# RMS norm with ReLU on one core: two pairs of transfers merged, and the work of VectorE and ScalarE rearranged around them

**Chip, cores, metric.** One core of one Trainium2 chip (trn2). The metric is the device time of one execution in microseconds (us), as the median of several runs. The span in a profile, from the first to the last instruction of the core, is about 1.3 us shorter than the time of the same run (157.9 against 159.28 us). All runs quoted here were at a granted clock of 1.000.

## The reference

```python
def reference(x, gamma, eps):              # x: 16 x 1024 x 512 float32, gamma: 512, eps: 1e-5
    rms = np.sqrt(np.mean(x ** 2, axis=-1, keepdims=True) + eps)
    x_norm = x / rms * gamma
    return np.maximum(x_norm, 0).astype(np.float32)
```

16384 rows of 512 floats go in and out: 33.55 MB each way, 67.11 MB in all.

## The kernel before

Each of the 128 partitions gets 128 rows, in 8 chunks of K = 16 rows; a group is G = 8 rows. The kernel keeps six chunks in memory on the chip ("slots"); chunks 6 and 7 take the places of chunks 0 and 1 once these are stored. SyncE issues all loads (L) and stores (S) of x and the result on one queue, in the order listed. A chunk's rows lie next to each other in device memory, so a transfer of r rows per partition moves as 128 packets of r x 2 KB (the packet records of this kernel: 512 of 16 KB, 1280 of 32 KB and 256 of 64 KB for 16 transfers).

```python
    order = [(L, 0, G), (L, G, G)] + [(L, i * K, K) for i in range(1, nslots)] + [
        (S, 0, K), (S, K, K), (L, room, K), (L, room + K, K),
        (S, 2 * K, 2 * K), (S, 4 * K, 2 * K), (S, room, K),
        (S, room + K, G), (S, room + K + G, G)]
    # ... SyncE, before each transfer m of the list:
        if kind == S:
            if order[m - 1][0] == L:
                nc.sync.wait_ge(*((tick, 6) if a == 0 else (done, 10)))
            nc.sync.wait_ge(done, (a + r) // G)
        elif a >= room:
            take(nc.sync, sems[order.index((S, a - room, r))], 16)   # room is free
        transfer(m)
```

ScalarE sums the squares of each row and takes roots, one group per turn of a loop of 16 (ring indices cut):

```python
        nc.scalar.wait_ge(ready, 1)                    # a group has landed
        for j in range(G):
            a = nc.scalar.activation(out=junk[:, j, :], in_=..., func=ACTF.Square, accum_out=ss[...])
        a.then_inc(sa, 1)
        nc.scalar.wait_ge(sa, 1)
        nc.scalar.activation(out=rms[...], in_=ss[...], func=ACTF.Sqrt,
                             bias=eps_sb, scale=inv_d).then_inc(sq, 1)
        nc.scalar.sem_inc(sa, -1)
        nc.scalar.sem_inc(ready, -1)
```

VectorE treats chunks 0 to 2 in a loop by group (cut), chunks 3 to 7 in long passes, one product with the reciprocals and one with gamma that also clamps at zero:

```python
    for first, last in ((3, 3), (4, 5), (6, 7)):
        nc.vector.wait_ge(sq, per * (last + 1 - looped))
        whole(nc.vector.reciprocal, ...)               # for chunks first..last
        nc.vector.wait_ge(sv, steps)
        for i in range(first, last + 1):
            blk = here(i * K, K)
            whole(nc.vector.tensor_tensor, out=blk, in0=blk, in1=rstd[...], op=ALU.mult)
            nc.vector.wait_ge(sv, steps)
            r = G if i == nchunks - 1 else K
            for a in range(i * K, (i + 1) * K, r):
                nc.vector._custom_dve(dve_ops.TENSOR_MUL_SAT, ...).then_inc(done, r // G)
```

## Time and profile before

| | before |
|---|---|
| median time | 159.34 us (159.28 to 159.47, 3 runs) |
| span of the profiled run | 157.9 us |
| VectorE (DVE) / ScalarE (ACT) busy | 86% / 55% of the span |
| queue of x and result (q1) busy on 16 DMA engines | 99.0% of the span |
| VectorE's last work ends | 150.54 us after the start of the span |

### The profile page before, as it was taken

The page shows a single profiled execution, that of the slowest core. Times are in us where ns is not written, and L with a number is a line of the kernel's source. Part 1 is how long each engine was busy: PE and PEld are TensorE (multiplying, and loading weights), DVE is VectorE, ACT ScalarE, POOL GpSimd, SP SyncE. Part 2 cuts the span into 40 slices and gives each one's busy share as a digit, 9 for nine tenths or more (in the row PEclk, how much of TensorE's full clock was granted, in tenths as well). Part 3 has the DMA queues.
Part 4 walks back from the last instruction along what each step waited for, and adds up shares of the span by engine and source line. Part 5 has one row for each costly group of instructions (what it writes and reads, how often), then busy time and mean ns, then how long its engine had stood idle before and what let it go on. Part 6 is the DMA issues. An engine that isn't in the chain of part 4 may idle for free.

```text
span 157.9 us, 770 instructions
## 1 busy us (share of the span) xinstructions
DVE 135.2 (86%) x76; ACT 86.3 (55%) x273; POOL 0.8 (0%) x6
## 2 busy tenths in 40 slices
DVE  0015999999999999999979999999999999999910
ACT  0298739989988988988920198898600000000000
POOL 1000000000000000000000000000000000000000
DMA  7999999999999999999999999996998969999997
GB/s 257 429 494 415 398 448 473 407 398 473 456 398 398 473 456 398 398 473 456 398 398 456 465 407 398 531 531 266 531 432 365 531 299 498 398 398 415 436 411 332
DMA packets 2313, 67.12 MB, mean 425 GB/s; under 512 B 261, under 2 KB 261, under 8 KB 265
## 3 DMA queue, kind: packets, MB, share of 16 engines
q1 hardware_dynamic: 2304, 67.11, 99.0%
q10 hardware_dynamic: 8, 0.01, 0.0%
q14 instruction: 1, 0.00, 0.0%
HBM read 33.56 MB, written 33.55 MB: 425 GB/s over the span
## 4 chain that ended last, share of the span: by engine, by line
DVE 44%; ACT 27%; issue 6%; ACTq 4%; DVEq 0%; POOLq 0%
ACT junk L137 26%; DVE slots L191 22%; DVE slots L174 22%; ACTq L137 3%; ACTq L132 1%; DVE rstd L174 0%; ACT rms L142 0%; ACTq L142 0%; ACTq L145 0%; DVEq L187 0%; POOLq L124 0%
## 5 line engine op out<-in xcount | busy, mean ns | idle before, releaser
L137 ACT ACTIVATE junk<-slots 128x512 f32 x128 | 74.4, 581 | 21.5 <-POOLq L124 17.0
L191 DVE CUSTOM_DVE_ANT_1 slots<-slots,gamma_sb 128x8192 f32<-128x8192 f32 (+1 forms) x6 | 43.5, 7269 | 0.6
L174 DVE TENSOR_TENSOR slots<-slots,rstd 128x8192 f32<-128x8192 f32 x5 | 43.4, 8689 | 0.1
L160 DVE SCALAR_TENSOR_TENSOR slots<-slots,rstd,gamma_sb 128x512 f32 x48 | 32.3, 747 | 0.9 <-DVE rstd L155 0.9
L137 ACT ACTIVATION_READ_ACCUMULATOR junk<-slots x128 | 23.9, 187 | 0.0
L167 DVE TENSOR_SCALAR slots<-slots x6 | 13.8, 2294 | 0.2
L148 DVE LOAD_MASK_SELECT gamma_sb<-gseed x1 | 0.0, 14 | 8.4 <-DMA gseed<-in_gamma_dram 8.4
L142 ACT ACTIVATE rms<-ss,eps_sb x16 | 4.8, 301 | 1.8
L155 DVE RECIPROCAL rstd<-rms x6 | 1.2, 196 | 4.3 <-ACT rms L142 4.3
L130 ACT ACT_TABLE_LOAD x1 | 1.3, 1283 | 3.6 <-issue 3.6
L174 DVE RECIPROCAL rstd<-rms 128x32 f32<-128x32 f32 (+1 forms) x3 | 0.9, 314 | 0.9 <-ACT rms L142 0.9
L148 DVE STREAM_SHUFFLE gamma_sb<-gseed 128x512 f32<-128x512 f32 x1 | 0.7, 716 | 0.0
L119 POOL MEMSET gseed<- 128x512 f32 x1 | 0.5, 526 | 1.5 <-POOLq L95 1.5
L220 POOL MEMSET const-bfloat16-1.0<- 128x1 bf16 x1 | 0.1, 103 | 0.0
L220 POOL MEMSET const-uint8-127<- 128x1 uint8 x1 | 0.1, 102 | 0.0
L220 POOL MEMSET const-float32-0.0<- 128x1 f32 x1 | 0.1, 100 | 0.2 <-issue 0.2
L220 POOL MEMSET const-float32-1.0<- 128x1 f32 x1 | 0.1, 100 | 0.0
L120 POOL MEMSET eps_sb<- 128x1 f32 x1 | 0.1, 99 | 0.0
## 6 DMA issues: line engine op xcount, KB each, us to landing
slots<-in_x_dram SPq DMA_DIRECT2D x7, 4096.0 KB, 29.4
out_dram<-slots SPq DMA_DIRECT2D x3, 4096.0 KB, 15.0
slots<-in_x_dram SPq DMA_DIRECT2D x2, 2048.0 KB, 9.6
out_dram<-slots SPq DMA_DIRECT2D x2, 2048.0 KB, 7.1
out_dram<-slots SPq DMA_DIRECT2D x2, 22.2
gseed<-in_gamma_dram ACTq DMA_DIRECT2D x1, 8.0 KB
```

Source lines behind the costliest of these rows:

```text
L119: nc.gpsimd.memset(gseed, 0.0).then_inc(sem_z, 1)
L130: nc.scalar.preload_act_table(ACTF.Sqrt)
L132: with nc.scalar.Fori(0, ngroups) as gi:
L137: a = nc.scalar.activation(out=junk[:, j, :], in_=slots[:, bass.ds(base + j * d, d)], func=ACTF.Square, accum_out=ss[:, bass.ds(col + j, 1)])
L142: nc.scalar.activation(out=rms[:, bass.ds(col, G)], in_=ss[:, bass.ds(col, G)], func=ACTF.Sqrt, bias=eps_sb, scale=inv_d).then_inc(sq, 1)
L148: nc.vector.stream_shuffle(gamma_sb, gseed, [0] * 32)
L155: nc.vector.reciprocal(out=rstd[:, bass.ds(col, G)], in_=rms[:, bass.ds(col, G)]).then_inc(sv, 1)
L160: r = nc.vector.scalar_tensor_tensor(out=row, in0=row, scalar=rstd[:, bass.ds(col + j, 1)], in1=gamma_sb, op0=ALU.mult, op1=ALU.mult)
L167: nc.vector.tensor_scalar_max(out=blk, in0=blk, scalar1=0.0).then_inc(done, 1)
L174: emit(**kw).then_inc(sv, 1)
L191: nc.vector._custom_dve(dve_ops.TENSOR_MUL_SAT, out=blk, in0=blk, in1=gamma_sb[:, None, :].to_broadcast([P, r, d]), s0=float("inf"), s1=0. ...
L220: nc = _bacc.Bacc("TRN2", target_bir_lowering=False, num_devices=1)
```

## The change

Its intent is to move the same bytes in fewer, longer packets: chunks 4 and 5 are loaded by one transfer (64 KB packets instead of 32), and chunk 7 is stored by one (32 KB instead of 16). The rest: reciprocals of chunks 4 and 5 apart, ScalarE scales the last 8 rows of chunk 7 in VectorE's stead, and ScalarE's loop loses two semaphore steps. The diff, cut to its core:

```diff
-    order = [(L, 0, G), (L, G, G)] + [(L, i * K, K) for i in range(1, nslots)] + [
+    order = [(L, 0, G), (L, G, G)] + [
+        (L, K, K), (L, 2 * K, K), (L, 3 * K, K), (L, 4 * K, 2 * K),
         (S, 0, K), (S, K, K), (L, room, K), (L, room + K, K),
-        (S, 2 * K, 2 * K), (S, 4 * K, 2 * K), (S, room, K),
-        (S, room + K, G), (S, room + K + G, G)]
+        (S, 2 * K, 2 * K), (S, 4 * K, 2 * K), (S, room, K), (S, room + K, K)]
 ...  (ScalarE: table load ahead of gamma's copy, eps under its own semaphore)
-                func=ACTF.Square, accum_out=ss[:, bass.ds(col + j, 1)])
+                func=ACTF.Square, accum_out=rms[:, bass.ds(col + j, 1)])
+            if j == 0:
+                a.then_inc(ready, -1)
         a.then_inc(sa, 1)
-        nc.scalar.wait_ge(sa, 1)
-        nc.scalar.activation(out=rms[...], in_=ss[...], ...).then_inc(sq, 1)
-        nc.scalar.sem_inc(sa, -1)
-        nc.scalar.sem_inc(ready, -1)
+        take(nc.scalar, sa, 1)
+        nc.scalar.activation(out=rms[...], in_=rms[...], ...).then_inc(sq, 1)
 ...
-    for first, last in ((3, 3), (4, 5), (6, 7)):
+    half = rows - G
+    for first, last in ((3, 3), (4, 4), (5, 5), (6, 7)):
 ...
+        if last == nchunks - 1:
+            nc.scalar.wait_ge(sv, steps)
+            for a in range(half, rows):
+                row = here(a, 1)
+                m = nc.scalar.activation(out=row, in_=row, func=ACTF.Identity,
+                                         scale=rstd[:, a:a + 1])
+            m.then_inc(am, 1)
 ...  (chunk 7: VectorE waits for am, multiplies its first 8 rows alone,
 ...   and makes one gamma pass over all 16 instead of two over 8)
```

## The prediction

> **What bounds the kernel now.** I read first the head of the page and its line of queues.
>
> ```profile
> span 157.9 us, 770 instructions
> DVE 135.2 (86%) x76; ACT 86.3 (55%) x273; POOL 0.8 (0%) x6
> ...
> DMA  7999999999999999999999999996998969999997
> ...
> q1 hardware_dynamic: 2304, 67.11, 99.0%
> ```
>
> The busiest engine, VectorE, works 86% of the span; the queue that carries x in and the result out (q1) works 99.0% of the span on all 16 DMA engines, 156.3 of 157.9 us. The sixes in the DMA row look like holes. To see whether they are, I asked for longer stretches, in the view of busy time by stretch (columns: stretch, length, busy DVE, ACT and POOL, clock, DMA share, GB/s).
>
> ```profile
> 2.00:60.00 58.00, 46.23 (x62) 46.63 (x146) 0.47 (x2) 1.00 1.01 433
> 60.00:98.00 38.00, 36.72 (x8) 25.59 (x84) 0.00 (x0) 1.00 1.02 436
> 98.00:138.00 40.00, 39.70 (x6) 14.08 (x46) 0.00 (x0) 1.00 1.00 433
> ```
>
> Shares of 1.00 to 1.02 and 433 to 436 GB/s in all three: no holes. A row moves as one packet of up to 64 KB, a packet lasts 0.6 to 2.4 us and is counted in the slice where it begins, so 4-us slices flicker. The first stretch holds loads alone, the last almost only stores, the middle both: the rate does not depend on the direction. From 2 us to the end the 16 engines are full, and the span is bytes over rate plus a start (DMA share 0.55 in the first 2 us) and the last landing.
>
> The chain that ended last says something else:
>
> ```profile
> DVE 44%; ACT 27%; issue 6%; ACTq 4%; DVEq 0%; POOLq 0%
> ```
>
> It follows semaphores from the last store's issue back to the work before it and cannot see that the store queued behind others. The timeline of SyncE and VectorE at the end shows this (start, length, engine, line, operation):
>
> ```profile
> 133.06 8.69 DVE L174 TENSOR_TENSOR slots<-slots,rstd 128x8192 f32<-128x8192 f32 x1
> ...
> 141.78 8.76 DVE L191 CUSTOM_DVE_ANT_1 slots<-slots,gamma_sb 128x4096 f32<-128x4096 f32 x2
> ...
> 146.23 0.33 SPq L83 DMA_DIRECT2D out_dram<-slots  x1
> ...
> 150.56 0.33 SPq L83 DMA_DIRECT2D out_dram<-slots  x1
> ```
>
> VectorE ends at 150.54 and the last 2 MB store is issued at 150.56. The page's list of issues has 7.1 us from issue to landing for these two stores, whereas 2.10 MB at 433 GB/s are 4.8 us. The remaining 2.3 us are start-up, queue and receipt. The stores are issued just early enough to keep the engines full; VectorE need be no earlier.
>
> [...]
>
> **Part 1, packets.** In the DMA view by stretch q1 stands as packets, MB, share of 16 engines, for 12 to 97 us (32 KB rows only), 100 to 136 us (64 KB rows) and 148 to 157 us (16 KB rows):
>
> ```profile
> q1 hardware_dynamic: 1248, 36.70, 100.3%
> ...
> q1 hardware_dynamic: 256, 15.73, 100.9%
> ...
> q1 hardware_dynamic: 251, 3.85, 100.3%
> ```
>
> Bytes over row size are 1120, 240 and 235 data packets; the rest are tiny semaphore packets, one per engine and transfer. Share x length x 16 / packets: 1.218, 2.422 and 0.615 us each. So two 32 KB packets take 2.436 us against 2.422 for one of 64 KB, two of 16 KB 1.230 against 1.218. The joined load replaces 16 packets of 32 KB per engine by 8 of 64 KB: 8 x 0.014 = 0.11 us. The whole last store replaces 16 of 16 KB by 8 of 32 KB: 8 x 0.012 = 0.10 us. Shares are rounded to 0.1%, so the sum of 0.2 us may be 0.1. This is all of the change that lies on the path. q1 should then show 1792 data packets + 14 x 16 = 2016 for the same 67.11 MB.
>
> **Part 2, VectorE's chain.** Now:
>
> ```profile
> 70.38 8.69 DVE L191 CUSTOM_DVE_ANT_1 slots<-slots,gamma_sb 128x8192 f32<-128x8192 f32 x1
> 80.00 0.35 DVE L174 RECIPROCAL rstd<-rms 128x32 f32<-128x32 f32 x1 [0.93 <-ACT rms L142]
> 80.39 8.69 DVE L174 TENSOR_TENSOR slots<-slots,rstd 128x8192 f32<-128x8192 f32 x1
> ```
>
> Chunks 4 and 5 share a reciprocal, which waits 0.93 us for chunk 5. Split, chunk 4's reciprocal follows at once: its product starts at about 79.27 instead of 80.39 (-1.12), and the second reciprocal gives back 0.28. Chunk 7's product shrinks to 4096 elements: 8.69 - 4.42 = -4.27; one whole gamma pass for two halves -0.07, less some gap. VectorE thus ends 5.1 us earlier, at about 145.45.
>
> **Part 3, ScalarE.** Its cycle per group is now 5.80 us (first squares at 28.17, 33.97, 39.77). Two semaphore steps leave it, 0.15 us in all; the in-place root saves memory and no pass. Against this the joined load lands chunk 4 with chunk 5, near 61 us rather than 51. Groups 8 to 11 then run about 61.2 to 84. Chunk 4's roots come near 72.5 and VectorE wants them at 79.0; chunk 5's near 84, wanted at 96.7. Groups 12 to 15 start with the load of chunk 6 as now (90.3) and end near 112.7, wanted at 114.4. None reaches VectorE. The 8 new scalings start at about 114.8, after the reciprocal of chunks 6 and 7, and take 8 x 0.61 = 4.9 us, to 120; VectorE wants them at 132.2, 12 us later. The root's table in front of gamma's copy swaps 1.3 us before gamma, which VectorE needs only at 13.4.
>
> **Part 4, the last store.** It waits for all of chunk 7: issued at 145.5. Now its first half is issued at 146.23, and the engines stay full over it: from 137.5 to 157.5 us, where all packets of the stores of chunks 6 and 7 lie, 8 x 1.218 + 16 x 0.615 = 19.6 us of packets per engine stand in 20.0 us, less the 0.4 us by which the engines are out of step. So the issue is some 0.7 us earlier than one known to be early enough, and brings 9.7 us of work instead of 4.8. The first store (57.72) hangs on a loop on VectorE that is unchanged.
>
> Sum: -0.2 us of packets, 0 from VectorE, 0 from ScalarE: 159.34 - 0.2 = **159.15 us**.
>
> **Rivals.** (a) VectorE's chain sets the end, as the view of the chain suggests. Then the last store starts at 145.5 and takes 1.0 us to its first packets (like the first load: issue at 0.0, DMA share 0.55 over 2 us), 9.7 us of data and 0.4 us of receipt: span 156.6, time about 158.0. Against it: the store of chunk 6 still holds the engines then: the 16 packets of 0.615 us per engine that follow it end at the end of the span, so begin near 147.5. (b) The whole store is late: if ScalarE's rows, the joined load or the reciprocals hold VectorE until t past 146.2, the engines idle for t - 146.2. If the 4.3 us saved were all lost, VectorE would end at 149.8 and the time be about 163 (+2.3%). Against it: the margins of 12, 6 and 1.7 us above; the 1.7 us is the thinnest. (c) 64 KB packets are slower as loads than as stores, which no row here shows: 1% slower over 19.4 us costs 0.2 us and eats the gain. Equal rates of loads and stores at 32 KB speak against it. (d) The joined load starves ScalarE for some 5 us near 56 to 61 us: true, and hidden.
>
> **Range and chances.** The step on the path is 0.1 to 0.2 us; runs of one kernel spread over 0.19 us (159.28 to 159.47). With that noise and a little for (a), (b) and (c) I take 158.85 to 159.45. Faster by 2% would need 156.15 us, less than the 156.3 us for which the engines are busy: 0.005. Slower by 2% needs 162.5, that is (b) almost in full: 0.01. The rest, 0.985, is within 2%.
>
> **What would show it.** Right: q1 at 2016 packets and again about 99% busy; last VectorE work ending near 145.5 (5 us earlier) with the span within 0.4 us of 157.9; issue to landing of the last store near 12 us; ScalarE idle near 56 to 61 us without VectorE waiting after it. Wrong: DMA share under 1 in the stretch 138 to 150 us (b), a VectorE wait for the scaled rows or for roots after 80 us (b), packets of 64 KB above 2.43 us in the load (c), or a span that follows VectorE down to 156.6 (a).

Two figures in the parts have these measured ones:

- 4.42 us for a product of 4096 elements (part 2). In the trace of the kernel before, the gamma pass takes 8.693 us for 8192 elements and 4.421 us for 4096 (means of L191 by shape), and the product 8.689 us for 8192. The product of 4096 itself is in the changed kernel's trace alone, with 4.42 us.
- 0.61 us from one scaling to the next (part 3). No trace showed it when it was written. In the changed kernel eight scalings take 5.01 us and one 0.708 us, so they start 0.61 us apart.

Three more measured numbers for what the prediction says without one. A packet is counted where it begins: in the changed kernel, from 41 to 58 us, slices of 0.43 us stand between 0 and 2313 GB/s, with q1 at 99.7% over the whole. The 0.4 us of receipt are the time from the end of the last packet (157.50 us) to the end of the span (157.95) in the trace before. And of the 2.3 us for start-up, queue and receipt that trace shows no more than this; from the issue to the first packet it was 0.8 us in late_5 below.

## The result

The changed kernel took 159.27 us (median of 6 runs, 159.10 to 159.62), the kernel before 159.32 us in the same rounds. The ratio is 0.9997 (95% interval 0.9984 to 1.0011). Ratios here are the mean time of one kernel's fast runs over that of the other's of the same rounds, so not quite the ratio of the medians.

The page of the changed kernel, in the lines that answer to the first ones of the prediction:

```profile
span 157.8 us, 744 instructions
...
DVE 130.9 (83%) x76; ACT 91.3 (58%) x281; POOL 0.8 (0%) x6
...
DMA  7999999999969979999999999996998969999996
...
q1 hardware_dynamic: 2016, 67.11, 99.0%
```

288 packets fewer for the same megabytes, VectorE 4.3 us less busy, ScalarE 5.0 us more, and the span 0.1 us shorter. The busy time by stretch shows engines as full as before:

```profile
2.00:60.00 58.00, 46.29 (x62) 43.70 (x137) 0.47 (x2) 1.00 1.01 435
60.00:98.00 38.00, 37.62 (x9) 28.78 (x92) 0.00 (x0) 1.00 1.01 434
98.00:138.00 40.00, 39.58 (x7) 18.75 (x53) 0.00 (x0) 1.00 1.00 433
```

VectorE's timeline: the second reciprocal follows without the wait of 0.93 us, and the last pass starts at 136.72 and ends at 145.42, 5.12 us earlier than before.

```profile
78.94 0.25 DVE L175 RECIPROCAL rstd<-rms 128x16 f32<-128x16 f32 x1
79.22 8.69 DVE L175 TENSOR_TENSOR slots<-slots,rstd 128x8192 f32<-128x8192 f32 x1
...
132.18 4.42 DVE L175 TENSOR_TENSOR slots<-slots,rstd 128x4096 f32<-128x4096 f32 x1
136.72 8.69 DVE L201 CUSTOM_DVE_ANT_1 slots<-slots,gamma_sb 128x8192 f32<-128x8192 f32 x1
```

ScalarE stands still for 5.09 us before group 8, since chunk 4 now lands with chunk 5, and scales its eight rows from 114.75 to 119.76, which VectorE wants at 132.18. Nobody waits for either:

```profile
61.07 0.60 ACT L138 ACTIVATE junk<-slots 128x512 f32 x1 [5.09 <-POOLq L126]
...
114.75 5.01 ACT L188 ACTIVATE slots<-slots,rstd 128x512 f32<-128x512 f32 x8 [2.22 <-DVE rstd L175]
```

In the DMA view of the end, the columns are KB per transfer and us from issue to landing. The last store is issued at 145.44 and takes 12.3 us to land; before, the two last stores took 7.1 us each.

```profile
out_dram<-slots SPq DMA_DIRECT2D x1, 4096.0 KB, 12.3
```

And the chain that ended last now gives VectorE an even larger share than the 44% of before:

```profile
DVE 64%; issue 8%; DVEq 2%; ACT 0%
```

A reader who took this view for the bound would have expected 5.12 us off the end to show. It did not.

### The profile page after: what moved, and what is told of

Read it like the earlier page. It is cut to its first block, busy times and chain, and to the rows that moved or that the text cites. A ratio compares the mean times of both kernels' runs of the same rounds, so it can differ in the third digit from the quotient of the medians.

```text
span 157.8 us, 744 instructions
## 1 busy us (share of the span) xinstructions
DVE 130.9 (83%) x76; ACT 91.3 (58%) x281; POOL 0.8 (0%) x6
## 3 DMA queue, kind: packets, MB, share of 16 engines
q1 hardware_dynamic: 2016, 67.11, 99.0%
## 4 chain that ended last, share of the span: by engine, by line
DVE 64%; issue 8%; DVEq 2%; ACT 0%
DVE slots L201 28%; DVE slots L175 25%; DVE slots L161 11%; DVEq L161 1%; DVE rstd L175 1%; DVE rstd L156 1%; DVEq L151 0%; ACT rms L145 0%; DVEq L156 0%; DVE slots L168 0%; DVEq L200 0%; DVEq L170 0%
## 5 line engine op out<-in xcount | busy, mean ns | idle before, releaser
L201 DVE CUSTOM_DVE_ANT_1 slots<-slots,gamma_sb 128x8192 f32<-128x8192 f32 x5 | 43.5, 8692 | 0.7
L175 DVE TENSOR_TENSOR slots<-slots,rstd 128x8192 f32<-128x8192 f32 (+1 forms) x5 | 39.2, 7837 | 0.1
L188 ACT ACTIVATE slots<-slots,rstd 128x512 f32<-128x512 f32 x8 | 5.0, 708 | 2.2 <-DVE rstd L175 2.2
L145 ACT ACTIVATE rms<-rms,eps_sb x16 | 4.8, 301 | 2.0
L175 DVE RECIPROCAL rstd<-rms 128x16 f32<-128x16 f32 (+1 forms) x4 | 1.1, 271 | 0.0
```

The source lines that it names most:

```text
L145: nc.scalar.activation(out=rms[:, bass.ds(col, G)], in_=rms[:, bass.ds(col, G)], func=ACTF.Sqrt, bias=eps_sb, scale=inv_d).then_inc(sq, 1)
L175: emit(**kw).then_inc(sv, 1)
L188: m = nc.scalar.activation(out=row, in_=row, func=ACTF.Identity, scale=rstd[:, a:a + 1])
L201: nc.vector._custom_dve(dve_ops.TENSOR_MUL_SAT, out=blk, in0=blk, in1=gamma_sb[:, None, :].to_broadcast([P, K, d]), s0=float("inf"), s1=0. ...
```

## The experiments

There were twelve runs. In all of them the last pass of VectorE is written as a scalar_tensor_tensor (max with 0, then times gamma) in place of the custom operation; gamma is all ones here, and all results were correct. "Before" and "changed" with this stand-in are the two controls. Each run was timed against the kernel before in the same rounds. The runs lie on four chips, on which the kernel before took 159.41 to 159.55 us in the median, so a difference of 0.1 us between runs of two chips is not to be read.

| run | what it is | median us | ratio to the kernel before (95%) |
|---|---|---|---|
| before_std | kernel before, stand-in | 159.45 | 0.9996 (0.9981 to 1.0012) |
| after_std | changed kernel, stand-in | 159.26 | 0.9991 (0.9977 to 1.0004) |
| after_std_2 | the same again | 159.32 | 0.9995 (0.9982 to 1.0008) |
| join_alone | before + joined load | 162.95 | 1.0218 (1.0203 to 1.0234) |
| whole_alone | before + whole last store | 162.86 | 1.0212 (1.0197 to 1.0228) |
| ve_alone | changed, transfers of before | 159.52 | 1.0000 (0.9983 to 1.0016) |
| loop_alone | before + ScalarE's loop | 159.57 | 0.9999 (0.9982 to 1.0016) |
| late_1 | changed, VectorE 0.4 us later | 159.29 | 0.9982 (0.9966 to 0.9999) |
| late_5 | changed, VectorE 2.6 us later | 160.37 | 1.0056 (1.0040 to 1.0073) |
| rows_16k | changed, all packets 16 KB | 160.82 | 1.0088 (1.0058 to 1.0118) |
| rows_8k | changed, all packets 8 KB | 161.85 | 1.0152 (1.0135 to 1.0169) |
| rows_2k | changed, all packets 2 KB | 174.91 | 1.0977 (1.0958 to 1.0995) |

Two theories are at stake. **DMA theory**: the engines are full, only the number of packets and gaps in their stream count. **VectorE's chain**: the end of VectorE's work sets the end.

### The controls

```diff
-                nc.vector._custom_dve(dve_ops.TENSOR_MUL_SAT, out=blk, in0=blk, in1=..., s0=float("inf"), s1=0.0)
+                nc.vector.scalar_tensor_tensor(out=blk, in0=blk, scalar=0.0, in1=...,
+                                               op0=ALU.max, op1=ALU.mult)
```

> Control. The kernel before, with its last VectorE pass (gamma and clamp in one custom operation) written as a scalar_tensor_tensor (max with 0, times gamma), the form that all experiments use. Every theory: same time as the kernel before, 159.3 us within 0.3; VectorE's last work ends near 150.5 us, at most 0.5 later, and the DMA engines stay full.

> Control. The changed kernel with the same stand-in. DMA theory (packets alone count): 159.2 us, within 0.3 of the kernel before; busy time of the data queue about 0.15 us less than in before_std; VectorE ends near 145.5. Rival (VectorE's chain sets the end): near 158.0.

Both as the DMA theory has it. The stand-in lasts as long as the custom operation (8.69 us for 8192 elements), and VectorE ended at 150.52 and 145.21 us. The packets' own times, summed from the packet records of the trace, are 156.26 us per engine in before_std and 156.07 in after_std: 0.19 us less, where about 0.15 was expected. The controls are fair.

### VectorE's part alone

```diff
 (changed kernel, stand-in)
-    order = [(L, 0, G), (L, G, G)] + [
-        (L, K, K), (L, 2 * K, K), (L, 3 * K, K), (L, 4 * K, 2 * K),
+    order = [(L, 0, G), (L, G, G)] + [(L, i * K, K) for i in range(1, nslots)] + [
         (S, 0, K), (S, K, K), (L, room, K), (L, room + K, K),
-        (S, 2 * K, 2 * K), (S, 4 * K, 2 * K), (S, room, K), (S, room + K, K)]
+        (S, 2 * K, 2 * K), (S, 4 * K, 2 * K), (S, room, K),
+        (S, room + K, G), (S, room + K + G, G)]
```

> The changed kernel with the transfers of before (single loads, last store in halves): only VectorE's and ScalarE's share of the change is left. VectorE ends near 145.5, 5 us earlier than before. DMA theory: no gain, 159.3 us within 0.3. Rival (VectorE's chain sets the end): about 5 us less, near 154 to 155, or at least below 158.

159.52 us, ratio 1.0000. VectorE's last pass of this run:

```profile
136.66 8.69 DVE L201 SCALAR_TENSOR_TENSOR slots<-slots,gamma_sb 128x8192 f32<-128x8192 f32 x1
```

It ends at 145.36, more than 5 us earlier than in before_std, and the time does not move. The rival falls: VectorE's chain is not what sets the end. Both halves of the last chunk are now stored at once, at 145.4, and only queue for longer (10.2 us to landing in the median instead of 7.5 in before_std).

### ScalarE's loop alone

```diff
 (kernel before, stand-in; ScalarE's loop and start as in the change)
+                func=ACTF.Square, accum_out=rms[:, bass.ds(col + j, 1)])
+            if j == 0:
+                a.then_inc(ready, -1)
-        nc.scalar.wait_ge(sa, 1)  ...  nc.scalar.sem_inc(sa, -1); nc.scalar.sem_inc(ready, -1)
+        take(nc.scalar, sa, 1)
```

> The kernel before with ScalarE's part of the loop alone: root in place, groups counted down on the first square, table load ahead of gamma's copy. DMA theory: ScalarE's cycle per group falls from 5.80 to about 5.65 us, the time stays 159.3 within 0.2. Rival (ScalarE is on the path, 27% of the chain): up to 16 x 0.15 = 2.4 us less.

159.57 us, ratio 0.9999. The cycle from root to root fell from 5.80 us (27.50 to 33.30 before) to 5.65 us (27.52 to 33.17). This also took away VectorE's wait of 0.93 us ahead of the shared reciprocal, which I had not foreseen: with the loop of 0.15 us less per group, chunk 5's roots are there in time.

```profile
79.03 0.35 DVE L174 RECIPROCAL rstd<-rms 128x32 f32<-128x32 f32 x1
```

In this kernel VectorE ends 1.04 us earlier than in before_std (149.48 against 150.52), again for nothing: the rival's 2.4 us do not appear.

### The joined load alone

```diff
 (kernel before, stand-in)
-    order = [(L, 0, G), (L, G, G)] + [(L, i * K, K) for i in range(1, nslots)] + [
+    order = [(L, 0, G), (L, G, G)] + [
+        (L, K, K), (L, 2 * K, K), (L, 3 * K, K), (L, 4 * K, 2 * K)] + [
```

> The kernel before with the joined load of chunks 4 and 5 and nothing else. DMA theory: chunk 4 lands with chunk 5 near 61 us, ScalarE starts group 8 near 61.2 instead of 57.2 and ends group 11 near 84.4; the shared reciprocal of chunks 4 and 5 waits for that, VectorE stands still some 5.3 us instead of 0.9 and finishes chunk 4 near 102.3; the store of chunks 2 and 3, which is held back until then, finds the engines empty from 98.8 on: about 4.5 us of gap, time near 163.7. Rival (a joined load saves its packets and is hidden otherwise): 159.2.

162.95 us, 2.2% slower. The mechanism is the expected one: VectorE's wait for the shared reciprocal of chunks 4 and 5 grows from 0.99 us in before_std to 4.92 us, and the store of chunks 2 and 3, which SyncE holds back until chunk 4 is done, is issued at 101.81 us instead of 97.96.

```profile
83.90 0.35 DVE L175 RECIPROCAL rstd<-rms 128x32 f32<-128x32 f32 x1 [4.92 <-ACT rms L143]
```

The busy time by stretch of join_alone shows the hole, with half the engines' time empty:

```profile
98.00:103.00 5.00, 5.00 (x2) 4.52 (x15) 0.00 (x0) 1.00 0.51 216
```

where before_std has none:

```profile
98.00:103.00 5.00, 5.00 (x1) 4.52 (x16) 0.00 (x0) 1.00 1.00 433
```

The size was 3.5 us instead of 4.4: the store was issued 0.5 us earlier than I had put it, and I had measured the gap from the first engine that runs dry, where the average over the 16 engines counts (3.74 us of idle time by the packet records of the trace).

So the joined load by itself costs 3.5 us. In the changed kernel the wait is gone: chunk 4's reciprocal needs chunk 4's roots alone and starts at 78.94 without one. That the split of the reciprocals does this, and not ScalarE's shorter loop, is worked out (four groups shorter by 0.15 us each make 0.6 us, and the wait was 4.92 us); no run leaves the split alone out.

### The whole last store alone

```diff
 (kernel before, stand-in)
-        (S, 2 * K, 2 * K), (S, 4 * K, 2 * K), (S, room, K),
-        (S, room + K, G), (S, room + K + G, G)]
+        (S, 2 * K, 2 * K), (S, 4 * K, 2 * K), (S, room, K), (S, room + K, K)]
```

> The kernel before with the whole last store and nothing else. DMA theory: the store waits for all of chunk 7, is issued at 150.6, its first packets run near 151.5, the engines have been empty since about 147.5: 4.0 us of gap, less 0.1 us of packets, time near 163.2. Rival (the last store's issue is hidden): 159.2.

162.86 us, 2.1% slower. VectorE is done at 150.38, the store is issued at 150.41, and until then nothing is left to move. From the busy time by stretch of whole_alone:

```profile
147.00:152.00 5.00, 3.38 (x1) 0.00 (x0) 0.00 (x0) 1.00 0.25 105
```

and of before_std:

```profile
147.00:152.00 5.00, 3.52 (x1) 0.00 (x0) 0.00 (x0) 1.00 0.98 416
```

So the second merged transfer also costs 3.4 us by itself. It is free in the changed kernel, where VectorE ends 5.1 us earlier. By the timeline, 4.3 us of this come from the eight rows that ScalarE scales and the rest from the wait that is gone; no run takes one of them alone out of the changed kernel.

### How late may the last store be?

```diff
 (changed kernel, stand-in; n = 1 or 5, in front of the last gamma pass)
+            if i == nchunks - 1:
+                nc.vector.tensor_tensor(
+                    out=junk[:, :n, :], in0=gamma_sb[:, None, :].to_broadcast([P, n, d]),
+                    in1=gamma_sb[:, None, :].to_broadcast([P, n, d]), op=ALU.mult)
```

> The changed kernel with one more VectorE operation of 512 elements per partition (about 0.6 us) ahead of the last pass. DMA theory: the last store is issued near 146.0, its first packets come 0.95 us later, the engines are free from about 147.1 on: the slack of some 0.7 us covers it, time unchanged (within 0.2). Rival (VectorE's chain sets the end): 0.6 us more.

> The same with 2560 elements (about 2.8 us). DMA theory: last store issued near 148.2, packets from 149.2, engines empty since 147.15 to 147.6: 2.0 us more than the changed kernel, near 161.2. Rival (VectorE's chain sets the end): 2.8 us more. Rival (stores are queued far ahead): no change.

late_1 moved VectorE's end from 145.21 to 145.62 us and the time not at all (159.29 us). late_5 moved it to 147.82, 2.6 us later, and the time by 1.1 us (160.37 against 159.26 us of after_std). The added operation itself lasted 0.69 us (512 elements) and 2.83 us (2560). The rest, 1.5 us, was slack, twice what I had put. The landing times of the last store show most of it, first in after_std, then in late_5:

```profile
out_dram<-slots SPq DMA_DIRECT2D x1, 4096.0 KB, 12.5
```

```profile
out_dram<-slots SPq DMA_DIRECT2D x1, 4096.0 KB, 11.1
```

In late_5 the store finds the engines empty and takes 11.1 us, as in whole_alone, which also has 11.1. In after_std it takes 1.4 us more, which is about the time it stood in the queue behind the store of chunk 6. This is a way to read slack here, within some 0.2 us (the changed kernel itself has 12.3, that is 1.2): issue to landing, less the same for a store that queued behind nothing.

### What a packet costs

```diff
 (changed kernel, stand-in; q = 8, 4 or 1 rows of 2 KB per packet)
-            "(p k) d -> p k d", k=k)[:, a - first:a - first + r, :]
-        ends = (there, here(a, r)) if kind == S else (here(a, r), there)
+            "(j p q) d -> p j (q d)", p=P, q=q)[:, (a - first) // q:(a - first + r) // q, :]
+        inside = here(a, r).rearrange("p (j q) d -> p j (q d)", q=q)
+        ends = (there, inside) if kind == S else (inside, there)
```

> The changed kernel with every load and store of x and the result cut into runs of 8 KB in device memory (another mapping of rows to partitions, the same in and out, so the result is right). Packet theory: a packet takes about 0.0085 us + 0.0377 us per KB (from 0.611, 1.2135 and 2.4185 us for 16, 32 and 64 KB), 512 packets of 0.310 us per engine make 158.6 us where the changed kernel's sizes make 155.2: 3.4 us more, near 162.6. Rival (bytes alone count): 159.2.

> The same with runs of 2 KB. Packet theory: 2048 packets of 0.084 us per engine make 171.6 us: 16.4 us more, near 175.6. Rival (bytes alone count): 159.2. Rival (short packets cost more than the line says): above 180.

> The changed kernel with all runs cut to 16 KB, to see the cost of a packet at the sizes that the change itself moves between. From the runs of 8 KB and 2 KB: 2.59 us for 400 more packets per engine is 6.5 ns, 15.65 us for 1936 is 8.1 ns. Here an engine has 256 packets instead of 112. Packet theory: 144 x 6.5 to 8.1 ns = 0.9 to 1.2 us more than the changed kernel, so 160.2 to 160.4 and a ratio of about 1.005 to 1.006. Rival (long packets have no cost of their own, only short ones): 159.3, ratio 0.999.

> The changed kernel with the stand-in again, as the partner on the same chip. Packet theory: 16 packets per engine fewer than before, 0.10 to 0.13 us less, ratio about 0.9992 to the kernel before; rival (the change as a whole is nothing): 1.0000. One run of this length cannot tell them apart alone (interval about 0.0013 each way); it adds to the others.

The packets of q1, with the tiny ones that count semaphores up (14 transfers x 16 = 224 in each; the pages have 228 packets under 512 B), from the pages of rows_16k, rows_8k and rows_2k in this order:

```profile
q1 hardware_dynamic: 4320, 67.11, 98.8%
```

```profile
q1 hardware_dynamic: 8416, 67.11, 99.7%
```

```profile
q1 hardware_dynamic: 32992, 67.11, 102.7%
```

Data packets are 4096, 8192 and 32768, that is 256, 512 and 2048 per engine, against 112 in the changed kernel. Over after_std's 159.26 us (after_std_2's 159.32 for rows_16k) the times are 1.50, 2.59 and 15.65 us longer, for 144, 400 and 1936 more packets per engine: 10.4, 6.5 and 8.1 ns for each. The first of these is uncertain, as the runs of rows_16k spread from 160.35 to 161.85 us; with its fastest run against the fastest of after_std_2 (159.17) it is 8.2 ns. So a packet has a cost of its own of 6.5 to 10 ns at these sizes. These runs also change which rows lie in which partition, and so the order of addresses, and no run separates this from the packet's size. But the durations from which my line was made (0.611, 1.2135 and 2.4185 us) come from traces without that change, and give 8.5 ns. "Bytes alone count" falls. My line for rows_8k (3.4 us) was too steep, that for rows_2k (16.4 us) close.

The change saves 16 packets per engine: 16 x 6.5 to 10.4 ns = 0.10 to 0.17 us.

## Why the prediction was right

Measured 159.27 us against 159.15 predicted and a range of 158.85 to 159.45; within 2%, as given at 0.985. The time alone is weak support: 159.34, no change at all, lies in the range too, and the measured difference (159.32 against 159.27) is within the noise. What speaks for the mechanism are the signs and the experiments. Step by step:

- **The bound.** Right, and shown: ve_alone and loop_alone take 5.2 and 1.0 us off VectorE's end with no effect, whereas join_alone and whole_alone open a gap in the stream of packets and pay for it at once. Rival (a) is refuted.
- **Packets, -0.2 us.** The count was right to the packet (2016). The size was at the lower end of what I gave: the 12 to 14 ns per packet of part 1 were too many, 6.5 to 10.4 ns measured make 0.10 to 0.17 us. The times alone cannot show it: the three runs of the changed kernel, with and without the stand-in, have ratios of 0.9997, 0.9991 and 0.9995, the three with the transfers of before 0.9996, 1.0000 and 0.9999, on average 0.0004 or 0.06 us apart, each with an interval of about 0.0013 either way (late_1, which has the changed transfers too, has 0.9982). In the trace's packet records it can be seen. The packets' times add up to 156.03 us per engine (changed), 156.07 (after_std), 156.05 (after_std_2) and 156.12 (late_1), against 156.23 (before), 156.26 (before_std), 156.23 (ve_alone) and 156.21 (loop_alone), 0.16 us less on average. The last 16 packets, about one for each engine, end in the median at 156.91, 157.02, 156.96 and 156.93 us in the first four, against 157.23, 157.22, 157.11 and 157.15 in the others. That is 0.2 us. But the span ends with the last engine, not the median one, and that one ended at 157.29, 157.30, 157.34 and 157.65 in the first four, at 157.50, 157.86, 157.71 and 157.82 in the others, 0.3 to 0.7 us behind the median. The gain shows for the typical engine, and at the end it is mostly drowned by how far the slowest one lags.
- **VectorE, 145.45.** Measured 145.42, with each term as worked out (4.42 us for the half product; start of chunk 4's product at 79.22 for 79.27).
- **ScalarE.** Group 8 started at 61.07 (61.2), the scalings ran 114.75 to 119.76 (114.8 to 120), one lasts 0.71 us and the next starts 0.61 us after it, and VectorE waited for none of it. The squares are 0.61 us apart too, but that gave no support to the figure for the scalings: between two squares (0.58 us) stands a read of the accumulator (0.19 us).
- **The last store.** No gap, as forecast (DMA share 1.01 from 138 to 150 us), and 12.3 us to landing for "near 12". The slack is 1.5 us by late_5. The "some 0.7 us" of the prediction were a lower bound, the distance to an issue known to be early enough; the mistake came after, when I took them for the slack itself and expected 161.2 us of late_5 (160.37). I had asked whether the first engine to run dry would be served in time. The average engine ends its packets later, the first packets came 0.8 us after the issue and not 1.0 (in late_5, issue at 147.84, first packet at 148.65), and after a gap the engines restart in step (in whole_alone the first 16 packets of the store begin between 151.20 and 151.40 us), so that the last one lags the median by 0.1 us at the end instead of 0.3 to 0.7.
- **Rival (b)** was the danger rightly named: about 163 us forecast if VectorE ended at 149.8; whole_alone, where it ended at 150.38, took 162.86. **Rival (c)**, slower 64 KB loads, did not occur: from 41 to 58 us, in the joined load, q1 stands at 112 packets, 7.34 MB and 99.7%, which is 2.421 us each, under the 2.43 named as the sign and equal to the 2.422 of the stores before.

What I had not put clearly is the structure of the change: it is two pairs. A merged load (8 packets per engine, 0.05 to 0.08 us, against 3.5 us of waiting) with its repair, the split reciprocals; and a merged store (the same prize, against 3.4 us) with its repair, ScalarE's rows and again the split. The two costs are measured, the pairing is worked out from them. Most of the code is repair. What stays open is why one engine lags behind the others at the end and why by a different amount in each run; the packet records kept here do not name the engine.

No version that beats both kernels came out of this. With the engines at 433 to 436 GB/s from 2 us on, what is left is the start, the landing, and some 0.9 us (112 packets x 8 ns) of packet costs; by the two merges above, further merging would delay a landing that VectorE needs or a store that frees room, but none was tried.

## What to carry to other kernels

When a queue is 99% busy on all engines, judge each part of a change by one question: does it open or close a gap in the stream of packets? Time taken off an engine that ends before the queue does was worth nothing here in itself (5.2 us in ve_alone, ratio 1.0000), but it can pay for another step, such as a larger store that must wait longer for its data (162.86 us in whole_alone, 159.27 in the changed kernel). Merging transfers saves only some 8 ns for each packet spared on an engine here, so first work out what the later landing or the later issue will cost: each of two such merges, done alone, lost forty times what it saved or more.

## What else the runs show

- The 4.19 MB store that finds the engines empty (late_5, whole_alone) takes 11.1 us to landing, of which 8 packets of 1.213 us are data. That leaves 1.4 us, 0.8 us of them ahead of the first packet.
- The 16 engines drift apart in a long stream. In 158 us the last one ended 0.3 to 0.7 us behind the median (1.2 us with 16 KB packets), which is of the size of the spread between one kernel's runs (159.10 to 159.62 us); that the one makes the other was not shown. After gaps of 1.3 us (late_5) to 3.9 us (whole_alone) they were in step again, within 0.2 us.
- A chain followed back along semaphores does not see a queue: here the chain gave VectorE 44% before and 64% after, and 5.1 us off VectorE's end moved the time by 0.05 us, which is within the noise. The time from issue to landing does see it (12.3 us in the queue, 11.1 us without one).
